# Half 0's four plain up-projection tiles become Strassen steps, with a new order of steps, sums and transfers around them

## The chip, the cores and the metric

The kernel runs on one core of one Trainium2 chip. The metric is the device time of one execution in microseconds, the median of several runs. "The profile" is one profiled execution, read as a page and through views of its trace; times within it count from the start of its span.

## The reference, cut to what matters

One layer of a hybrid encoder on 512 positions of 1024 features. The change touches the last block alone, and there the first product:

```python
x = x + mix @ w_out[l]
h = rms_norm(x, mlp_norm_g[l])                                  # 512 x 1024
x = x + jnp.square(jax.nn.relu(h @ w_up[l])) @ w_down[l]        # 1024 -> 4096 -> 1024
return rms_norm(x, final_norm_g)
```

## The kernel before

Every product is made in three passes, to reach float32 accuracy from fp32r matmuls: each operand is split into a rounded high part and the low part that is left, and `mm3` (L311) adds hi·hi, hi·lo and lo·hi into PSUM. The split of a weight chunk of 128x1024 is two instructions: ScalarE copies the high part (`conv_hi`, L240, instruction at L247), VectorE subtracts it to get the low part (`conv_lo`, L261, at L269). The order on TensorE, ScalarE, VectorE and GpSimd is the written order; SyncE's queue is put in order by a planner, except inside the attention loop.

The up projection runs in two halves of 16 output tiles (`for half in range(2)`, L1513), each followed by its part of the down projection. There are two kinds of tile work:

- A plain tile (`up_tile` L1558, and three tiles together at the start of half 0): 8 k-blocks of three matmuls with 512 columns, then two ReLUs from PSUM on ScalarE and, for every second tile, squares on VectorE (`up_evac`, L1312).
- A group of four tiles done as a 2x2 block product with Strassen's seven products. Each product is a step (`up_step`, L1574) of 8 x 3 matmuls with 256 columns. Steps are named `f0:kind`: 11 and 21 use unsummed weights and unsummed activations; t1, t2, t3 and t4 use sums of weight blocks, and t1, t2, t3 and 22 sums of activation blocks. A group has up to three PSUM banks: a (11, t2, t3, t4), b (21) and c (t1, 22). `quad_evac` (L1372) follows each step: ScalarE copies 11, t1 and t2 out as `v`, VectorE adds `v` and PSUM for t3, 21 and 22; the ReLU and the square come later, on ScalarE for groups in `ON_ACT`.

In half 0 tiles 0 to 3 are plain (`n0` to `n3` in `STEPS`, L54) and the groups 4, 8 and 12 are Strassen groups: 4 tiles and 21 steps. In half 1 all four groups are Strassen groups: 28 steps.

What surrounds the steps, in half 0:

- Weights. Unsummed chunks arrive in three rotating `wraw` buffers; `emit_dma` (L226) loads the next when one is used up. Summed weights live in four rotating `tw` buffers: `load_t` (L1177) loads block 12 through SyncE and adds further blocks with accumulating DMAs from GpSimd's queue (L1181). t1 becomes t2 in place by another accumulating DMA (L277), t3 gets block 22 added by VectorE (L281), and t4 is t2 + 21, added by VectorE (L286). During each step the weights of the third step after it are split (`feed`, L299).
- Activations. `h2_t` (L1207) transposes x1n on TensorE into PSUM, and ScalarE writes the high part h2h and a copy hm; `h2_l` (L1219) subtracts on VectorE. Four of these stand in the output projection (`BES`, L1242 on), four after the first k-block of the plain tiles. `h_sums` (L1330) then makes the four sums on VectorE, 16 instructions in all, and stores them in DRAM for half 1; `h_hi` and `h_lo` (L1356, L1360) split them.
- `x1_sq` (L1266) squares x1n for the norm, eight times in half 0; `scale_neg` (L1546) makes the negated factors. `load_s1` (L1498) brings and adds the first weights of the down projection into `ts`.
- `late` ties such work to a step and a k-block; `op_next` and `next_a` fill in sums and splits of the finished activations for the down projection.

## Time and profile before

| | us |
|---|---|
| Median of 3 runs | 525.5 (525.3 to 525.65) |
| The profiled execution's own time | 525.27 |
| Its span | 523.5 |
| Its mean granted TensorE clock | 0.997 of full speed |
| TensorE, VectorE, ScalarE busy | 516.8, 430.2, 352.3 |

In rows of the trace the columns are start, duration, engine, line, operation, the tiles written and read, and how often. A row that groups instructions has the summed busy time, the mean of one in ns, and the idle time of the engine before them with what ended it. Matmuls overlap in their pipeline: two rows' start times tell more than the durations. L312, L313 and L314 are the three passes of `mm3`. `pu` is PSUM of the up projection, `pd` that of the down projection, `pxt` that of the transposes. The time outside the span is 525.27 - 523.5 = 1.77.

### The profile page before, as it was taken

How to read it: one execution, taken by the hardware profiler on the slowest of the kernel's cores; microseconds unless marked ns; L12 is line 12 of the kernel's file. 1: busy time of each engine (PE TensorE's matmuls, PEld its weight loads, DVE VectorE, ACT ScalarE, POOL GpSimd, SP SyncE). 2: the span in 40 equal slices, each digit the busy share in tenths (PEclk: the TensorE clock that was granted, in tenths of full speed). 3: DMA queues.
4: the chain of work that ended last, by engine and by line, in shares of the span. 5: the costliest groups of instructions: out<-in, count | busy, mean ns of one | idle time of the engine just before them, and what ended most of it. 6: DMA issues, size and time to landing. Idle time of an engine off the chain costs nothing.

```text
span 523.5 us, 8213 instructions
## 1 busy us (share of the span) xinstructions
PE 516.8 (99%) x3021; PEld 443.4 (85%) x3021; DVE 430.2 (82%) x668; ACT 352.3 (67%) x568; POOL 65.8 (13%) x90
## 2 busy tenths in 40 slices
PE   9999999999999999999999999999999999999995
PEld 8857888787787788899999888889999999888884
DVE  6998995888887898898789987789766978986985
ACT  7579946668865847586578656565667577655664
POOL 0182000000000421001300311001100300140000
PEclk9999999999999999999999999999999999999998
DMA  7736545357696499947695899977987497799804
GB/s 288 234 87 196 161 145 180 106 168 216 187 289 208 104 191 268 332 133 192 140 222 149 217 273 275 308 265 162 294 260 172 115 229 208 156 283 257 202 1 162
DMA packets 40329, 105.15 MB, mean 201 GB/s; under 512 B 5056, under 2 KB 13376, under 8 KB 40288
## 3 DMA queue, kind: packets, MB, share of 16 engines
q1 hardware_dynamic: 32448, 78.10, 44.6%
q0 software_dynamic: 7696, 26.32, 27.2%
q8 instruction: 24, 0.39, 0.3%
q10 hardware_dynamic: 144, 0.20, 0.1%
q14 instruction: 17, 0.14, 0.1%
HBM read 95.59 MB, written 4.29 MB: 191 GB/s over the span
## 4 chain that ended last, share of the span: by engine, by line
PE 99%; DVE 0%; issue 0%; DVEq 0%; ACT 0%; ACTq 0%
PE pu L313 10%; PE pu L314 10%; PE pu L312 10%; PE pd L313 10%; PE pd L312 10%; PE pd L314 10%; PE pqk L312 3%; PE pwo L312 3%; PE pqk L314 3%; PE pqk L313 3%; PE pwo L314 3%; PE pwo L313 3%; PE pav L942 2%; PE pt L842 2%; PE ps L806 2%; PE pp L312 1%
## 5 line engine op out<-in xcount | busy, mean ns | idle before, releaser
L269 DVE TENSOR_TENSOR wlo<-wraw,whi 128x1024 fp32r<-128x1024 f32 x71 | 86.5, 1219 | 24.2 <-ACT whi L247 24.0
L247 ACT ACTIVATE whi<-wraw 128x1024 fp32r<-128x1024 f32 x67 | 70.7, 1057 | 37.3 <-PE pd L314 18.2
L313 PE MATMUL pd<-wlo,ah 128*128 128x512 f32 (+1 forms) x195 | 75.2, 386 | 0.0
L312 PE MATMUL pd<-whi,ah 128*128 128x512 f32 (+1 forms) x195 | 75.2, 386 | 0.0
L314 PE MATMUL pd<-whi,al 128*128 128x512 f32 (+1 forms) x195 | 75.2, 386 | 0.0
L314 PE MATMUL pu<-hh,wlo 128*128 128x256 f32 x224 | 63.4, 283 | 0.0
L313 PE MATMUL pu<-hl,whi 128*128 128x256 f32 x224 | 63.4, 283 | 0.0
L312 PE MATMUL pu<-hh,whi 128*128 128x256 f32 x224 | 63.4, 283 | 0.0
L312 PE MATMUL pu<-h2h,whi 128*128 128x256 f32 (+1 forms) x200 | 60.1, 300 | 0.0
L313 PE MATMUL pu<-h2l,whi 128*128 128x256 f32 (+1 forms) x200 | 60.0, 300 | 0.0
L314 PE MATMUL pu<-h2h,wlo 128*128 128x256 f32 (+1 forms) x200 | 60.0, 300 | 0.0
L269 DVE TENSOR_TENSOR wlo<-tw,whi 128x1024 fp32r<-128x1024 f32 x37 | 45.1, 1220 | 17.2 <-ACT whi L247 17.2
L247 ACT ACTIVATE whi<-tw 128x1024 fp32r<-128x1024 f32 x38 | 40.1, 1059 | 25.1 <-PE pd L314 6.3
L247 ACT ACTIVATE whi<-ts 128x1024 fp32r<-128x1024 f32 x24 | 25.5, 1061 | 26.5 <-PE pd L314 18.5
L312 PEld LDWEIGHTS pu<-hh,whi 128*128 128x128 f32 x224 | 43.0, 192 | 0.0
L313 PEld LDWEIGHTS pu<-hl,whi 128*128 128x128 f32 x224 | 43.0, 192 | 0.0
L314 PEld LDWEIGHTS pu<-hh,wlo 128*128 128x128 f32 x224 | 43.0, 192 | 0.0
L312 PEld LDWEIGHTS pd<-whi,ah 128*128 128x128 f32 x195 | 36.6, 188 | 7.4
L314 PEld LDWEIGHTS pd<-whi,al 128*128 128x128 f32 x195 | 36.6, 188 | 7.4
L313 PEld LDWEIGHTS pd<-wlo,ah 128*128 128x128 f32 x195 | 36.6, 188 | 7.3
L312 PEld LDWEIGHTS pu<-h2h,whi 128*128 128x128 f32 x200 | 38.3, 191 | 1.3
L313 PEld LDWEIGHTS pu<-h2l,whi 128*128 128x128 f32 x200 | 38.3, 191 | 1.3
(277 smaller groups left out, 1218.0 us busy)
## 6 DMA issues: line engine op xcount, KB each, us to landing
wraw<-in_w_up_dram SPq DMA_DIRECT2D x25, 512.0 KB, 4.8
ts<-in_w_dn_dram POOLq DMA_DIRECT2D x24, 512.0 KB, 13.1
wraw<-in_w_dn_dram SPq DMA_DIRECT2D x24, 512.0 KB, 8.9
tw<-in_w_up_dram SPq DMA_DIRECT2D x15, 512.0 KB, 6.6
tw<-in_w_up_dram POOLq DMA_DIRECT2D x15, 512.0 KB, 7.9
wraw<-in_w_in_dram SPq DMA_DIRECT2D x13, 512.0 KB, 3.9
ts<-in_w_dn_dram SPq DMA_DIRECT2D x8, 512.0 KB, 7.5
tw<-in_w_dn_dram SPq DMA_DIRECT2D x8, 512.0 KB, 7.5
```

Source lines behind the costliest of these rows:

```text
L247: act(hi, raws[i], AF.Copy)
L269: nc.vector.tensor_tensor(lo, r, f(splits[i][0]), op=OP.subtract)
L312: nc.tensor.matmul(o, lhsT=a[0], rhs=b[0], start=bool(first), stop=False, skip_group_check=on)
L313: nc.tensor.matmul(o, lhsT=a[0], rhs=b[1], start=False, stop=False, skip_group_check=on)
L314: nc.tensor.matmul(o, lhsT=a[1], rhs=b[0], start=False, stop=bool(last), skip_group_check=on)
L806: nc.tensor.matmul(psq[p, u][e][:, :NK], lhsT=qs_[p, a][r, P * qt:P * qt + P], rhs=kks[p][r, b, w:w + NK], start=i == 0, stop=i == 2)
L842: nc.tensor.transpose(pt[:, i * P:(i + 1) * P], en[h][qt][:, k:k + P], ident)
L942: nc.tensor.matmul(pav[p][a, co], lhsT=vs[:, jt, h * DH:(h + 1) * DH], rhs=et[h, jt][:, ci], start=jt == 0 and i == 0, stop=jt == 3 and i ...
```

## The change

- `STEPS[0]` has group 0 in place of the four plain tiles, so half 0 has 28 steps too. Its first six are 11 and 21 of the groups 0, 8 and 4, which need no sums. `up_tile`, `up_evac` and the three tiles at the start go.
- The first step takes its matmuls in another order: for each half of the output hi·hi and lo·hi of all four k-blocks, then the four that read the low activations.
- `h_sums` becomes `h_sum`, tied to steps one by one: the t1 and t2 sums on VectorE, the t3 and 22 sums on GpSimd (12 instructions). The later four transposes stand in the first and second step, in two lots.
- In half 0 all t4 weight sums are accumulating DMAs (`RAW`); group 0's t2 is loaded for itself and its t3 gets block 22 by DMA (`ADDED`); group 12's t3 gets it by VectorE one step later (`more`). `load_t` can leave its adds to `add_t`, at a later step.
- The evacuation of three 21 steps is put off (`later`, `put`); every group's squares are on ScalarE; group 4's bank a moves to other PSUM buffers (`AJ`).
- Four of the eight `x1_sq` and the negated factors move into the down projection. The adds of the first down weights (`add_s1`) stand apart from their loads, in the last steps.
- From the ninth step of half 0 to its last, SyncE's order is the written one.
- The second half of the final gain is loaded in three pieces in place of four (`FGP`).

```diff
 STEPS = (
-    "n0 n1 n2 4:11 4:t1 n3 4:t2 4:21 4:22 4:t3 8:11 8:t1 4:t4 8:21 8:t2 8:22 8:t3 12:11 12:t1 8:t4 12:t2 12:22 12:t3 12:21 12:t4",
+    "0:11 8:11 4:11 0:21 8:21 4:21 0:t1 8:t1 0:t2 0:22 0:t3 8:t2 4:t1 8:22 0:t4 8:t3 4:t2 8:t4 4:22 12:11 4:t3 12:t1 4:t4 12:t2 12:22 12:t3 12:21 12:t4",
     "0:11 0:t1 0:21 0:t2 0:22 0:t3 8:11 8:t1 0:t4 8:21 8:t2 8:22 8:t3 12:11 12:t1 8:t4 12:21 12:t2 12:22 12:t3 4:11 4:t1 12:t4 4:t2 4:22 4:t3 4:21 4:t4")
-QUADS = ((4, 8, 12), (0, 8, 12, 4))
-ON_ACT = {(h, f, k) for h in range(2) for f in QUADS[h] if (h, f) != (0, 4) for k in ("21", "22", "t3", "t4")}
+QUADS = ((0, 8, 4, 12), (0, 8, 12, 4))
+AJ = {(0, 4), (1, 0)}
+ADDED = {(0, 0), (0, 12)}
+RAW = {(0, 0), (0, 4), (0, 8), (0, 12)}
+ON_ACT = {(h, f, k) for h in range(2) for f in QUADS[h] for k in ("21", "22", "t3", "t4")}
...
     for (h, f0, kind), i in cq.items():
-        if kind == "11" and (h, f0) != (0, 4):
+        if kind == "11" and h:
+            swap[i], swap[i + 1] = i + 1, i
+        if (h, f0, kind) == (0, 12, "t2"):
...
                     raws[cq[h, f0, "t2"]] = r
-                elif kind == "22":
+                elif kind == "22" and (h, f0) not in ADDED:
...
                     nc.vector.tensor_tensor(t, t, r, op=OP.add)
+                elif kind == "22" and f0 == 12:
+                    st["r"] = r
+                elif (h, f0) in RAW and kind == "t2":
+                    nc.gpsimd.dma_start(r, ublock(h, "21", f0), accum_op=OP.add)
+                    raws[cq[h, f0, "t4"]] = r
+                elif (h, f0) in RAW and kind == "21":
+                    emit_dma()
...
-    def load_t(half, n, f0):
+    def load_t(half, n, f0, adds=True):
...
         nc.sync.dma_start(t, ublock(half, "12", f0))
-        for b in {"t1": ("11",), "t2": ("11", "22"), "t3": ()}[n]:
-            nc.gpsimd.dma_start(t, ublock(half, b, f0), accum_op=OP.add)
         raws[cq[half, f0, n]] = t
+        if adds:
+            add_t(half, n, f0)
+    def add_t(half, n, f0):
+        for b in {"t1": ("11",), "t2": ("11", "22"), "t3": ("22",) if (half, f0) in ADDED else ()}[n]:
+            nc.gpsimd.dma_start(raws[cq[half, f0, n]], ublock(half, b, f0), accum_op=OP.add)
...
     BES["21"].update({1: lambda: o_lo("s1", 1), 3: lambda: conv_lo(C_WA + 7)})
-    BES["s1"].update({1: lambda: (o_lo("22", 0), o_lo("22", 1), h2_t(0, "gs")), 2: lambda: h2_t(1, "gs"), 3: lambda: (conv_lo(C_WA + 8), h2_l(0))})
-    BES["22"].update({1: lambda: (h2_t(2, "gs"), h2_l(1)), 2: lambda: (h2_t(3, "gs"), conv_lo(C_WA + 9)), 3: lambda: (h2_l(2), h2_l(3))})
+    BES["s1"].update({1: lambda: (o_lo("22", 0), o_lo("22", 1), h2_t(0, "gs")), 2: lambda: h2_t(1, "gs"), 3: lambda: (h2_t(2, "gs"), h2_l(0))})
+    BES["22"].update({0: lambda: h2_l(1), 1: lambda: (h2_t(3, "gs"), h2_l(2)), 2: lambda: (h2_l(3), conv_hi(C_WA + 9)), 3: lambda: None})
...
                 BES[w][i]()
-        if w in ("s3", "s4", "21"):
-            load_t(0, {"s3": "t1", "s4": "t2", "21": "t3"}[w], 4)
+        if w in ("s3", "s4", "21", "s1"):
+            load_t(0, *{"s3": ("t1", 0), "s4": ("t3", 0, False), "21": ("t2", 0), "s1": ("t1", 8)}[w])
...
-    def h_sums(k):
+    def h_sum(n, k):
...
         if k % 2 == 0:
-            for n in SUMS:
-                hsum[n, m] = g_("hsum")
-        a, b = hm.pop(k), hm.pop(k + 4)
-        e, s2, s3, s4 = [hsum[n, m][:, c] for n in SUMS]
-        nc.vector.tensor_tensor(e, b[:, right], a[:, right], op=OP.subtract)
-        stt(s2, a[:, left], -1.0, e, op0=OP.mult, op1=OP.subtract)
-        nc.vector.tensor_tensor(s3, a[:, left], a[:, right], op=OP.subtract)
-        stt(s4, b[:, left], -1.0, s2, op0=OP.mult, op1=OP.subtract)
+            hsum[n, m] = hsr[n, m] = g_("hsum")
+        a, b, o = hm[k], hm.get(k + 4), hsr[n, m][:, c]
+        if n == "t1":
+            nc.vector.tensor_tensor(o, b[:, right], a[:, right], op=OP.subtract)
+        elif n == "t2":
+            stt(o, a[:, left], -1.0, hsr["t1", m][:, c], op0=OP.mult, op1=OP.subtract)
+        elif n == "t3":
+            nc.gpsimd.tensor_tensor(o, a[:, left], a[:, right], op=OP.subtract)
+        else:
+            nc.gpsimd.tensor_tensor(o, a[:, left], b[:, left], op=OP.subtract)
+            nc.gpsimd.tensor_tensor(o, o, hsr["t1", m][:, c], op=OP.add)
         if k % 2:
-            for i, n in enumerate(SUMS):
-                nc.sync.dma_start(hsd[i][:, m * S:(m + 1) * S], hsum[n, m])
+            nc.sync.dma_start(hsd[SUMS.index(n)][:, m * S:(m + 1) * S], hsr[n, m])
+    hsr = {}
...
     HJ = 20
-    FGP = ((0, 32, 64, 128), (0, 32, 64, 96, 128))
+    FGP = ((0, 32, 64, 128), (0, 32, 64, 128))
...
-    def load_s1(half, ts, qs=range(NQ)):
-        for q in qs:
-            t = ts[:, q, :]
-            nc.sync.dma_start(t, wblock(half, "11", q))
-            nc.gpsimd.dma_start(t, wblock(half, "12", q), accum_op=OP.add)
-            raws[cd_[half] + 2 * q + 1] = t
+    def load_s1(half, ts, q):
+        nc.sync.dma_start(ts[:, q, :], wblock(half, "11", q))
+    def add_s1(half, ts, q):
+        t = raws[cd_[half] + 2 * q + 1] = ts[:, q, :]
+        nc.gpsimd.dma_start(t, wblock(half, "12", q), accum_op=OP.add)
...
     for half in range(2):
-        c0, cd = cu.get((half, 0)), cd_[half]
+        cd = cd_[half]
...
         todo = deque((w, q) for _, w, q in seq)
...
-        def scale_neg():
+        def room():
...
             ts = big.tile([P, NQ, 1024], FT, name="ts", tag="bigA")
-            for tt in range(4):
-                nr2[tt] = consts.tile([P, 1], FT, name="nr2_%d" % tt)
-                nc.vector.tensor_scalar(nr2[tt], r2[tt], -1.0, None, op0=OP.mult)
...
             bank, keep = banks.setdefault(f0, {}), keeps.setdefault(f0, {})
-            x = {"t1": "c", "22": "c", "21": "b"}.get(kind, "a")
-            if x not in bank:
-                bank[x] = ps_("pu", {"a": "pj" if (half, f0) == (1, 0) else "gs", "b": "pj", "c": "et"}[x])
+            b = {"t1": "c", "22": "c", "21": "b"}.get(kind, "a")
+            if (half, kind, f0) == (0, "11", 4):
+                banks[0]["b"] = ps_("pu", "pj")
+            if b not in bank:
+                bank[b] = ps_("pu", {"a": "pj" if (half, f0) in AJ else "gs", "b": "pj", "c": "et"}[b])
...
             hi, lo = splits[c]
+            head = half == 0 and (kind, f0) == ("11", 0)
...
                 sl = slice(n * P, (n + 1) * P)
-                mm3(bank[x][:, e * TH:(e + 1) * TH], (hi[:, sl], lo[:, sl]), h_part(kind, k),
-                    n == 0 and kind in ("11", "t1", "21"), n == 7, True)
+                o, w, x, first = bank[b][:, e * TH:(e + 1) * TH], (hi[:, sl], lo[:, sl]), h_part(kind, k), n == 0 and kind in ("11", "t1", "21")
+                if head:
+                    nc.tensor.matmul(o, lhsT=w[0], rhs=x[0], start=first, stop=False, skip_group_check=True)
+                    nc.tensor.matmul(o, lhsT=w[1], rhs=x[0], start=False, stop=False, skip_group_check=True)
+                    for k in range(4) if n % 4 == 3 else ():
+                        sl = slice((4 * e + k) * P, (4 * e + k + 1) * P)
+                        nc.tensor.matmul(o, lhsT=hi[:, sl], rhs=h_part(kind, k)[1], start=False, stop=n == 7 and k == 3, skip_group_check=True)
+                else:
+                    mm3(o, w, x, first, n == 7, True)
...
                     op_next()
-                if n == 6:
+                if n == 6 and (half, kind, f0) != (0, "t2", 12):
                     next_a()
-            quad_evac(kind, f0, bank, keep, (half, f0, kind) in ON_ACT)
+            if half == 0 and kind == "21" and f0 < 12:
+                later.append(lambda: quad_evac("21", f0, bank, keep, True))
+            else:
+                quad_evac(kind, f0, bank, keep, (half, f0, kind) in ON_ACT)
+        later = deque()
+        def put():
+            later.popleft()()
...
                     ts = big.tile([P, NQ, 1024], FT, name="ts", tag="bigA")
-                load_s1(half, ts, (q,))
+                load_s1(half, ts, q)
+                if half:
+                    add_s1(half, ts, q)
...
         qs = QUADS[half]
-        for f0, f1 in zip(qs, qs[1:]):
+        for f0, f1 in zip(qs, qs[1:]) if half else ():
...
         if half == 0:
-            late.update({(4, "11", 0): split_h("t2", 0), (4, "11", 5): split_h("t2", 1), (4, "t1", 1): split_h("22", 0), (4, "t1", 6): split_h("22", 1),
-                         (3, 1): split_h("t3", 0), (3, 6): split_h("t3", 1),
-                         (4, "t1", 4): xt(0, 1), (3, 3): xt(1, 0), (4, "21", 4): xt(1, 1), (4, "t2", 4): xt(2, 0), (4, "22", 4): xt(2, 1),
-                         (4, "t3", 4): xt(3, 0), (8, "11", 5): xt(3, 1), (8, "21", 5): scale_neg})
+            def more():
+                t, r = raws[cq[0, 12, "t3"]], st.pop("r")
+                nc.vector.tensor_tensor(t, t, r, op=OP.add)
+            def sums(*a):
+                return lambda: [h_sum(n, k) for n, k in a]
+            def turn(js):
+                def run():
+                    for j in js:
+                        h2_t(j, "et" if j < 6 else "pj")
+                        h2_l(j)
+                return run
+            late.update({(0, "11", 0): lambda: conv_lo(C_WA + 8), (0, "11", 3): lambda: conv_lo(C_WA + 9), (0, "11", 6): turn((4, 5)), (8, "11", 1): turn((6, 7)),
+                         (0, "11", 1): sums(*[("t3", k) for k in range(4)]), (8, "11", 0): sums(("t1", 0), ("t1", 1)), (8, "11", 5): split_h("t1", 0),
+                         (4, "11", 0): sums(("t1", 2), ("t1", 3), ("22", 0), ("22", 1), ("22", 2), ("22", 3)),
+                         (4, "11", 1): split_h("t1", 1), (0, "21", 0): sums(("t2", 0), ("t2", 1)),
+                         (0, "21", 5): split_h("t2", 0), (8, "21", 0): sums(("t2", 2), ("t2", 3)), (8, "21", 5): split_h("t2", 1),
+                         (4, "21", 5): split_h("22", 0), (0, "t1", 5): split_h("22", 1),
+                         (0, "t3", 3): put, (8, "t2", 3): put, (8, "t1", 1): split_h("t3", 0), (0, "t2", 1): split_h("t3", 1),
+                         (8, "21", 2): lambda: load_t(0, "t1", 4, False), (4, "21", 2): lambda: add_t(0, "t1", 4), (8, "11", 7): lambda: add_t(0, "t3", 0),
+                         (8, "t1", 5): lambda: load_t(0, "t3", 8),
+                         (8, "t2", 6): lambda: load_t(0, "t3", 4), (0, "t4", 3): put, (8, "t3", 0): lambda: load_t(0, "t1", 12, False), (4, "t2", 2): lambda: add_t(0, "t1", 12),
+                         (4, "t3", 0): lambda: load_t(0, "t3", 12, False), (12, "t1", 7): more,
+                         (0, "22", 7): xt(0, 0), (8, "t2", 7): xt(0, 1), (8, "22", 7): xt(1, 0), (4, "t2", 5): xt(1, 1), (4, "22", 5): room,
+                         (12, "t1", 5): lambda: add_s1(half, ts, 0), (12, "t2", 5): lambda: add_s1(half, ts, 1), (12, "22", 5): lambda: add_s1(half, ts, 2), (12, "t3", 5): lambda: add_s1(half, ts, 3)})
...
         if half == 0:
-            late[8, "t3", 4], late[12, "11", 4], late[12, "t2", 1], late[12, "t2", 7] = [load_1(q) for q in range(4)]
+            late[4, "t3", 4], late[12, "11", 4], late[12, "t2", 1], late[12, "t2", 7] = [load_1(q) for q in range(4)]
...
             late[12, "t3", 4], late[4, "11", 4], late[4, "t2", 1], late[4, "t2", 7] = [load_1(q) for q in range(4)]
-        for kind, f0 in up_steps(half)[start:]:
+        for n, (kind, f0) in enumerate(up_steps(half)):
+            if half == 0 and n == 8:
+                sp = tc.manual_schedule(engines={nc.sync.engine})
+                sp.__enter__()
...
             st["step"] = st.get("step", 0) + 1
-            if kind == "n":
-                up_tile(f0, late)
-            else:
-                up_step(kind, f0, late)
+            up_step(kind, f0, late)
+        if half == 0:
+            sp.__exit__(None, None, None)
...
                 load_s3(half, q)
+            if half == 0 and j < 4:
+                x1_sq(2 + j // 2, j % 2)
+                nr2[j] = consts.tile([P, 1], FT, name="nr2_%d" % j)
+            if half == 0 and j == 4:
+                for tt in range(4):
+                    nc.vector.tensor_scalar(nr2[tt], r2[tt], -1.0, None, op0=OP.mult)
...
```

## The prediction

> **What bounds the kernel now.** I read the page first, for the share of each engine and the chain that ended last, then the busy time of the two up-projection stages, then TensorE's order of time at their edges.

> ```profile
> span 523.5 us, 8213 instructions
> PE 516.8 (99%) x3021; PEld 443.4 (85%) x3021; DVE 430.2 (82%) x668; ACT 352.3 (67%) x568; POOL 65.8 (13%) x90
> PE 99%; DVE 0%; issue 0%; DVEq 0%; ACT 0%; ACTq 0%
> ...
> 200.30:284.20 83.90, 83.90 (x616) 79.98 (x615) 71.31 (x107) 56.41 (x92) 6.94 (x8) 1.00 0.73 205
> 360.20:441.60 81.40, 81.40 (x677) 81.28 (x676) 62.20 (x68) 53.89 (x74) 8.64 (x10) 1.00 0.79 208
> ```

> The reader sees one chain, TensorE from end to end. The two last rows are the up-projection of half 0 and of half 1: span, busy time of PE, PEld, DVE, ACT and POOL, granted clock (1.00), DMA share. TensorE never idles there, so only fewer or shorter matmuls gain anything, and every other engine has room: VectorE 85% and 76%, ScalarE 67% and 66%.

> The start times of matmuls, not their modelled durations, give the price of a step.

> ```profile
> 200.30 0.40 PE L312 MATMUL pu<-h2h,whi 128*128 128x512 f32 x1
> ...
> 202.35 1.95 PE L1214 MATMUL pxt<-ident,x1n 128*128 128x128 f32 x16
> 204.06 0.48 PE L312 MATMUL pu<-h2h,whi 128*128 128x512 f32 x1
> 204.37 0.40 PE L313 MATMUL pu<-h2l,whi 128*128 128x512 f32 x1
> ...
> 284.37 0.40 PE L312 MATMUL pd<-whi,ah 128*128 128x512 f32 x1
> ...
> 360.55 0.28 PE L312 MATMUL pu<-h2h,whi 128*128 128x256 f32 x1
> ...
> 441.19 0.40 PE L312 MATMUL pd<-whi,ah 128*128 128x512 f32 x1
> ```

> Half 1 is already 28 Strassen steps: 441.19 - 360.55 = 80.64, or 2.88 a step, 24 matmuls of 256 columns at 0.120. Half 0 runs from 200.30 to 284.37 = 84.07: four plain tiles, 21 steps and 16 transposes. The steps are 60.48; the transposes take 204.06 - 202.35 = 1.71 and their next matmul 0.31 in place of 0.23; what is left for four plain tiles is 21.8, or 5.45 each (0.227 a matmul).

> **The change part by part.** *Matmuls.* Four plain tiles (21.8) become seven steps (20.16): -1.61 by the same difference taken without rounding, 84.07 - 80.64 - 1.82 for the transposes. This is on the path and is all that can be gained. The transposes are split into two lots of eight: one more restart, +0.08.

> *The first steps.* 0:11 now starts where n0 did and needs the fourth low part h2l. TensorE's first eight matmuls use only high parts, so the low parts are asked for at 200.30 + 8 x 0.12 = 201.26, the fourth at 201.6.

> ```profile
> 200.39 0.70 ACT L1217 ACTIVATE hm<-pxt,vt 128x512 f32<-128x512 f32 x1
> ...
> 201.64 0.75 DVE L1204 SCALAR_TENSOR_TENSOR x1n<-pwo,nrc,x 128x512 f32<-128x512 f32 x1
> ...
> L269 DVE TENSOR_TENSOR wlo<-wraw,whi 128x1024 fp32r<-128x1024 f32 x13 | 15.9, 1220 | 4.6 <-ACT whi L247 4.5
> L1387 DVE TENSOR_TENSOR a<-v,pu 128x512 f32<-128x512 f32 x9 | 6.1, 680 | 0.8 <-PE pu L314 0.7
> L1361 DVE TENSOR_TENSOR hl<-hsum,hh 128x512 fp32r<-128x512 f32 x8 | 5.2, 683 | 0.0
> L1220 DVE TENSOR_TENSOR h2l<-hm,h2h 128x512 fp32r<-128x512 f32 x7 | 4.7, 688 | 2.1 <-ACT hm L1217 2.1
> L286 DVE TENSOR_TENSOR tw<-tw,wraw 128x1024 f32<-128x1024 f32 x3 | 3.7, 1219 | 0.0
> L1320 DVE TENSOR_TENSOR a<-a 128x512 f32<-128x512 f32 x4 | 2.6, 684 | 0.0
> L1398 DVE SCALAR_TENSOR_TENSOR a<-a 128x512 f32<-128x512 f32 x3 | 2.1, 693 | 0.1
> L1337 DVE TENSOR_TENSOR hsum<-hm 128x256 f32<-128x256 f32 x4 | 1.7, 418 | 0.0
> ```

> Its source hm is there at 200.39 + 0.70 = 201.1, its subtraction takes 0.69: 201.8, so about +0.15. Behind it on VectorE stands the last x1n, which the moved transposes need at the seventh eighth of 0:11 (about 202.7): 201.8 + 0.75 = 202.5, in time.

> The two weight splits that stood in the output projection (1.22 each, VectorE) are moved into 0:11, behind that x1n. The tightest point is then 4:21, the sixth step. It starts at 200.30 + 0.15 + 5 x 2.88 + 2 x 0.86 of transposes = 216.6. Up to its low weights VectorE must do, from 201.1: five h2l (3.4), one x1n (0.75), five wlo (6.1), four sums for t1 (1.7), two hl (1.4), together 13.4, ready about 214.5, 215.1 with the waits for ScalarE. Slack 1.5. The steps before it have 0.8 (8:11) to 3 (8:21). So the new head hides, if nothing is added to VectorE; I put +0.2 for small misses.

> *Sums of activations by GpSimd.* Four sums for t3 and eight instructions for "22" leave VectorE (8 x 0.42 = 3.4 off it) and become twelve 128x256 tensor_tensors on GpSimd. No row has one of that size. The tiny ones show what matters:

> ```profile
> 29.51 0.20 POOL L163 TENSOR_TENSOR pl<-pl,z 128x8 f32<-128x8 f32 x1
> 30.12 0.53 POOL L163 TENSOR_TENSOR pl<-pl,z 128x8 f32<-128x8 f32 x1
> 30.74 0.73 POOL L164 TENSOR_SCALAR pl<-pl 128x8 f32<-128x8 f32 x1
> ...
> 30.63 0.75 DVE L504 SCALAR_TENSOR_TENSOR xc<-xr,vt,xc 128x511 f32<-128x511 f32 x1
> 31.42 0.75 DVE L505 SCALAR_TENSOR_TENSOR xc<-xr,vt,xc 128x511 f32<-128x511 f32 x1
> 32.09 0.74 DVE L503 SCALAR_TENSOR_TENSOR xc<-xr,vt,xc 128x510 f32<-128x510 f32 x1
> 32.87 0.75 DVE L504 SCALAR_TENSOR_TENSOR xc<-xr,vt,xc 128x511 f32<-128x511 f32 x1
> ```

> Beside VectorE instructions with two operands in SBUF the same GpSimd instruction grows from 0.20 to 0.53 to 0.73: it waits its turn. VectorE starts come 0.67 or 0.78 apart, so a turn costs it about 0.11. Bounds for a 128x256 one: 0.24 (as the tiny ones) to 0.84 (twice VectorE's 0.418); I take 0.6. What VectorE loses lies between nothing (they fall in its waits) and all twelve, 7.2. The likeliest case takes nothing more than the 0.2 above, since the first four read only hm of the first transposes and may run before the low weights are asked for, and the t2 and 22 parts are used only from the ninth step.

> [...]

> *The rest of half 0.* VectorE: +3 weight splits (3.7), +3 evacuations (2.0), less the squares of plain tiles (2.6), the squares now on ScalarE (2.8), the sums (3.4) and three t4 sums that become DMAs (3.7), less about 1 of moved scalars: 71.3 - 7.8 = 63.5 of 82.5, 77%. ScalarE: three weight copies, three v, six relu-and-square pairs more, less eight relus and four squares of x1n moved into the down projection:

> ```profile
> L247 ACT ACTIVATE whi<-wraw 128x1024 fp32r<-128x1024 f32 x12 | 12.8, 1070 | 2.3 <-PE pu L313 1.6 <-ACT scr L1269 0.7
> L1377 ACT ACTIVATE v<-pu 128x512 f32<-128x512 f32 x9 | 5.5, 606 | 6.3 <-PE pu L314 6.3
> L1396 ACT ACTIVATE a<-a 128x512 f32<-128x512 f32 x5 | 3.2, 632 | 0.2
> L1269 ACT ACTIVATE scr<-x1n 128x512 f32<-128x512 f32 x8 | 5.0, 629 | 0.0
> L1317 ACT ACTIVATE a<-pu 128x256 f32<-128x256 f32 x8 | 2.5, 389 | 1.0 <-PE pu L314 1.0
> ```

> about 56.4 + 8 = 64 of 82.5, 78%. Half 1 hides the same steps at 76% and 66%, so on the average nothing shows: 0. The price without that cover is the 1.1 to 1.2 of one split for each step that is late.

> *Transfers and queues.* Each group's t4 sum, and t2 and t3 of group 0, become accumulating DMAs on POOL: eight more of 512 KB. POOL issues in order, so an add that waits for its load holds those behind it; SP in written order does the same.

> ```profile
> DMA to landing us min/median/max: 4.6/6.6/9.8
> ...
> DMA to landing us min/median/max: 5.3/8.8/13.3
> ...
> DMA to landing us min/median/max: 5.4/5.4/7.9
> ...
> tw<-in_w_up_dram POOLq DMA_DIRECT2D x2, 512.0 KB, 6.5
> ```

> These are the loads of line 1179, the adds of 1181, those of 277, and the adds between 230 and 240. The late one is group 12. With step s starting at 202.2 + 2.88 s, its t1 buffer is free when 8:t4 is split, at 202.2 + 14 x 2.88 + 0.7 + 2.3 = 245.5; load 5.0, add 6.5, two conversions 2.3, add 5.4, conversions 2.3 end at 267.0; 12:t2 starts at 268.4. Slack 1.4 by those; by the medians of 6.6 and 8.8 it is 2.5 late; by the minima 3 early. I take 0, the middle of the two ends. While a transfer is late ScalarE waits, and evacuations and copies behind it.

> Moved squares and scale factors go to the first four turns of the down projection, where ScalarE is under two thirds busy; the four w_down adds go to the last steps, and one final-gain load is dropped: 0.

> Sum: -1.61 + 0.08 + 0.15 + 0.2 = -1.2. Against the profiled execution's 525.27 that is 524.1; the median shown is 0.23 higher, so 524.3.

> **The rivals.** *VectorE and GpSimd take turns in the head.* Four t3 sums and four of the 22 sums fall before the low weights of 4:21: 8 x 0.6 = 4.8, less the slack of 1.5 and 0.7 spent in VectorE's own waits: 2.6 late at 4:21, 526.9, slower. It decides from the point where more than 1.5 is lost before 4:21. For it: the rows at 30 us, and a full VectorE there; against it: sums that may run early.

> *The add of group 12 is late.* Half of the 2.5 by medians, 1.3: 525.6, no change. For it: the medians; against it: half 1 has the same pairs and its longest wait for such a transfer is short and hidden:

> ```profile
> ACT whi L247 <- DMA tw<-in_w_up_dram: 4.8, 2, 2.6
> ```

> *SyncE's written order or the POOL queue holds a load back,* so that the saving is not reached and several steps wait: both stalls together and one more, 3.7, 528.0. Against it: buffers of raw weights are still asked for three chunks ahead.

> **How the numbers follow.** What this kernel's measurement can tell from no change is about 0.2%, 1.05. Chances: forecast 0.48 (524.3), first rival 0.25 (526.9), second 0.17 (525.6), third 0.10 (528.0). Faster by over 0.2% is below 524.45: 0.43 of the first case and 0.02 of the second rival where the add comes early, 0.45. Slower, above 526.55: 0.20 + 0.03 + 0.10 = 0.33. The rest, 0.22, lies between. The full saving with no miss is 523.9, so the range starts at 523.8; it ends at 527.6, which leaves out most of the last case. The forecast's own range is 523.8 to 525.0.

> **What would show it.** TensorE from the first to the last up matmul of half 0 should be 82.5 to 82.9 in place of 84.07. If the first rival holds, GpSimd's sums read 0.6 or more, VectorE's starts spread beside them, and TensorE waits at 4:21 for wlo. If the second holds, TensorE waits at 12:t1 or 12:t2, and ScalarE's whi waits for a tw transfer over 4. A stall-free half 0 with a time above 525 would make the prediction wrong elsewhere: in the down projection, where I priced everything at nothing.

## The result, and the profile after

The changed kernel takes **535.07 us** (median of 5 runs, 532.46 to 535.23) against 525.6 (525.3 to 526.15) for the kernel before on the same chip: 1.0168 times, 95% interval 1.0154 to 1.0182. It is slower by 9.5 us, and the forecast of 524.3 and its range were wrong. The profiled execution took 534.54, its span is 532.5.

In the changed kernel the three passes of `mm3` are L320 to L322, the first step's matmuls L1545 to L1549, a weight's high and low part L248 and L270. First the page: span, busy time of the engines, and the chain that ended last.

```profile
span 532.5 us, 8398 instructions
...
PE 519.0 (97%) x3093; PEld 447.6 (84%) x3093; DVE 429.5 (81%) x655; ACT 361.4 (68%) x581; POOL 82.6 (16%) x109
...
PE 82%; DMA 6%; DVE 5%; issue 3%; ACT 2%; POOL 0%; DVEq 0%; ACTq 0%; POOLq 0%; SPq 0%
```

The chain was TensorE from end to end; now 6% of it is a transfer, 5% VectorE, 2% ScalarE. The new kernel's busy time does not tell where; what TensorE waited for between 200 and 297 does (engine, tile and line, what it waited for; us in total, times, the longest):

```profile
PE pd L320 <- ACT a L1383: 3.6, 1, 3.6
PE pu L320 <- DVE a L1386: 1.3, 2, 1.1
PE pu L1549 <- DVE h2l L1232: 1.3, 2, 1.1
PE pu L322 <- DVE wlo L270: 0.7, 1, 0.7
```

The kernel before had none of these four. The up projection's first matmul starts at 201.00 and the first of the down projection at 287.84, 86.84 where 82.5 was forecast, so 4.3 of stalls, not quite half of the loss (between starts a stall costs somewhat more than the wait shown: 4.2 for the four that follow, against 3.3 above). They are, in order: 1.8 in the first step for the low activations h2l, 0.8 at 4:21 for its low weights, 0.4 and 1.2 for two evacuations (the moving of a result out of PSUM) at 240 and 256. The largest stands behind them, in the second turn of the down projection:

```profile
289.00 0.39 PE L322 MATMUL pd<-whi,al 128*128 128x512 f32 x1
292.95 0.79 PE L320 MATMUL pd<-whi,ah 128*128 128x512 f32 x1 [3.56 <-ACT a L1383]
```

And it costs twice. Rows by stretch are: span, busy time of PE, PEld, DVE, ACT, POOL, the granted clock, the DMA share, GB/s.

```profile
288.90:292.90 4.00, 0.49 (x3) 0.06 (x1) 3.52 (x5) 3.94 (x8) 0.85 (x1) 1.00 1.06 236
293.00:295.00 2.00, 2.00 (x5) 1.62 (x6) 1.97 (x4) 1.97 (x4) 0.00 (x0) 0.50 1.06 213
295.00:297.00 2.00, 2.00 (x8) 1.57 (x7) 1.97 (x4) 2.00 (x5) 0.00 (x0) 0.65 1.05 231
297.00:299.00 2.00, 2.00 (x10) 1.64 (x9) 2.00 (x4) 1.78 (x5) 0.00 (x0) 1.00 1.02 307
```

After the wait the granted clock is 0.50: the next eight matmuls start 0.43 apart in place of 0.23, which takes another 1.7. The sum over the kernel: matmuls 82.5 - 84.07 = -1.6, stalls in the up projection +4.3, the wait at its end +3.7, slow clock +1.7, and +0.7 that is already there at the first up matmul (201.00 against 200.30). It is there from the kernel's first loads on, in code that the change leaves alone: the first matmul into the tile `pcs` starts at 21.09 against 20.37. That is +8.8 of 532.5 - 523.5 = 9.0. After 300 the two run alike.

**Why ScalarE's ReLU was 3.6 late.** ScalarE works in the written order. The copy ahead of that ReLU for which it waited, and the ReLU (six instructions between them are left out); then SyncE's issues before them; then SyncE's longest wait; then GpSimd's issue of the additions:

```profile
287.52 1.06 ACT L248 ACTIVATE whi<-ts 128x1024 fp32r<-128x1024 f32 x1 [6.66 <-DMA ts<-in_w_dn_dram]
292.32 0.58 ACT L1383 ACTIVATE a<-pu 128x512 f32<-128x512 f32 x1
```
```profile
257.49 0.43 SPq L1498 DMA_DIRECT2D ts<-in_w_dn_dram  x1
257.97 1.20 SPq L1187 DMA_DIRECT2D tw<-in_w_up_dram  x1
272.67 0.33 SPq L229 DMA_DIRECT2D wraw<-in_w_dn_dram  x1
273.04 1.27 SPq L1498 DMA_DIRECT2D ts<-in_w_dn_dram  x2
```
```profile
SPq L229 <- DVE tw L1598: 13.4, 1, 13.4
```
```profile
279.90 2.62 POOL L1502 DMA_DIRECT2D ts<-in_w_dn_dram  x3 [7.89 <-DMA ts<-in_w_dn_dram]
```

From 259 to 272.67 SyncE stands 13.4 at a `wraw` load whose buffer comes free only when VectorE has done `more`, the t3 sum of group 12. Two loads of `ts` stand behind it in the written order although their own place is free. They leave at 273.04. One of them is the first of the four: in the new order its place, 4:t3, stands one step behind that of the second, 12:11, which left at 257.49. GpSimd adds in the order of use, so the addition of the second, long loaded, waits behind the first too, and three go out together at 279.90. ScalarE waits 6.66 for the first sum, and the ReLU that frees the PSUM bank stands behind that copy in its order. The planner of the kernel before had issued all four at 202.41.

**Why the first step and 4:21 stalled.** The groups of VectorE and of GpSimd beside it, from 200.6 to 219 (count, busy, mean ns of one, idle before it), and from 199 to 219:

```profile
L1232 DVE TENSOR_TENSOR h2l<-hm,h2h 128x512 fp32r<-128x512 f32 x6 | 8.1, 1382 | 0.0
L270 DVE TENSOR_TENSOR wlo<-wraw,whi 128x1024 fp32r<-128x1024 f32 x5 | 6.8, 1392 | 0.8 <-ACT whi L248 0.8
L1360 DVE TENSOR_TENSOR hl<-hsum,hh 128x512 fp32r<-128x512 f32 x2 | 1.8, 911 | 0.7 <-ACT hh L1357 0.7
```
```profile
L1338 POOL TENSOR_TENSOR hsum<-hm 128x256 f32<-128x256 f32 x4 | 4.3, 1081 | 3.3 <-ACT hm L1229 3.3
L1339 POOL TENSOR_TENSOR hsum<-hsum 128x256 f32<-128x256 f32 x4 | 3.7, 932 | 4.0 <-DVE hsum L1332 3.8
L1336 POOL TENSOR_TENSOR hsum<-hm 128x256 f32<-128x256 f32 x4 | 3.1, 1059 | 0.0
```

An h2l subtraction takes 1382 ns where it took 688, a weight split 1392 where it took 1220, a split of sums 911 where it took 683: VectorE is held up while GpSimd's sums run, and a sum on GpSimd takes 0.93 to 1.08 (means).

**Why two evacuations stalled.** ScalarE's longest wait for summed weights in half 0:

```profile
237.33 1.06 ACT L248 ACTIVATE whi<-tw 128x1024 fp32r<-128x1024 f32 x1 [3.54 <-DMA tw<-in_w_up_dram]
```

With two more such waits, at 232.25 (2.47) and 240.54 (0.58), ScalarE has 6.6 less and works from there to 257 without a break, so its copies come late. At 253 VectorE waits 1.39 for one of them, adds a t3 sum (1.22) and only then makes the `a` that frees the bank at 256. The transfers are full meanwhile (share 1.06 from 232 to 240).

### The profile page after: what moved, and what is told of

Its sections match the earlier page's. It is cut to its first block, busy times and chain, and to the rows that moved or that the text cites. A ratio compares the mean times of both kernels' runs of the same rounds, so it can differ in the third digit from the quotient of the medians.

```text
span 532.5 us, 8398 instructions
## 1 busy us (share of the span) xinstructions
PE 519.0 (97%) x3093; PEld 447.6 (84%) x3093; DVE 429.5 (81%) x655; ACT 361.4 (68%) x581; POOL 82.6 (16%) x109
## 4 chain that ended last, share of the span: by engine, by line
PE 82%; DMA 6%; DVE 5%; issue 3%; ACT 2%; POOL 0%; DVEq 0%; ACTq 0%; POOLq 0%; SPq 0%
PE pd L320 10%; PE pd L322 9%; PE pd L321 9%; PE pu L320 6%; PE pu L322 6%; PE pu L321 6%; DMA tw<-in_w_up_dram 4%; PE pqk L320 3%; PE pqk L322 3%; PE pqk L321 3%; PE pwo L320 3%; PE pwo L322 2%; PE pwo L321 2%; PE pav L950 2%; PE pt L850 2%
## 5 line engine op out<-in xcount | busy, mean ns | idle before, releaser
L270 DVE TENSOR_TENSOR wlo<-wraw,whi 128x1024 fp32r<-128x1024 f32 x70 | 86.1, 1233 | 23.9 <-ACT whi L248 23.7
L248 ACT ACTIVATE whi<-wraw 128x1024 fp32r<-128x1024 f32 x66 | 69.3, 1054 | 35.2 <-PE pd L322 17.6
L320 PE MATMUL pd<-whi,ah 128*128 128x512 f32 (+1 forms) x195 | 75.9, 389 | 3.6 <-ACT a L1383 3.6
L322 PE MATMUL pd<-whi,al 128*128 128x512 f32 (+1 forms) x195 | 75.7, 388 | 0.0
L320 PE MATMUL pu<-hh,whi 128*128 128x256 f32 x256 | 72.5, 283 | 0.3 <-DVE a L1386 0.3
L321 PE MATMUL pu<-hl,whi 128*128 128x256 f32 x256 | 72.4, 283 | 0.0
L322 PE MATMUL pu<-hh,wlo 128*128 128x256 f32 x256 | 72.4, 283 | 0.0
L270 DVE TENSOR_TENSOR wlo<-tw,whi 128x1024 fp32r<-128x1024 f32 x41 | 50.1, 1221 | 23.3 <-ACT whi L248 23.3
L248 ACT ACTIVATE whi<-tw 128x1024 fp32r<-128x1024 f32 x42 | 44.3, 1056 | 24.7 <-DMA tw<-in_w_up_dram 10.9
L320 PE MATMUL pu<-h2h,whi 128*128 128x256 f32 x184 | 52.2, 284 | 1.1 <-DVE a L1386 1.1
L322 PE MATMUL pu<-h2h,wlo 128*128 128x256 f32 x184 | 52.2, 284 | 0.7 <-DVE wlo L270 0.7
L321 PE MATMUL pu<-h2l,whi 128*128 128x256 f32 x184 | 52.1, 283 | 0.0
L320 PEld LDWEIGHTS pu<-hh,whi 128*128 128x128 f32 x256 | 49.1, 192 | 0.4 <-ACT whi L248 0.4
L321 PEld LDWEIGHTS pu<-hl,whi 128*128 128x128 f32 x256 | 49.1, 192 | 0.0
L322 PEld LDWEIGHTS pu<-hh,wlo 128*128 128x128 f32 x256 | 49.1, 192 | 0.0
L320 PEld LDWEIGHTS pd<-whi,ah 128*128 128x128 f32 x195 | 36.9, 189 | 11.2 <-ACT a L1383 4.0
L248 ACT ACTIVATE whi<-ts 128x1024 fp32r<-128x1024 f32 x24 | 25.4, 1059 | 30.1 <-PE pd L322 15.8
L322 PEld LDWEIGHTS pd<-whi,al 128*128 128x128 f32 x195 | 36.9, 189 | 7.6
L270 DVE TENSOR_TENSOR wlo<-ts,whi 128x1024 fp32r<-128x1024 f32 x24 | 29.3, 1223 | 16.2 <-ACT whi L248 16.1
L320 PEld LDWEIGHTS pu<-h2h,whi 128*128 128x128 f32 x184 | 35.3, 192 | 1.3 <-ACT a L1394 1.3
## 6 DMA issues: line engine op xcount, KB each, us to landing
wraw<-in_w_up_dram SPq DMA_DIRECT2D x24, 512.0 KB, 4.9
wraw<-in_w_dn_dram SPq DMA_DIRECT2D x24, 512.0 KB, 9.6
ts<-in_w_dn_dram POOLq DMA_DIRECT2D x24, 512.0 KB, 11.8
tw<-in_w_up_dram POOLq DMA_DIRECT2D x22, 512.0 KB, 7.7
tw<-in_w_up_dram SPq DMA_DIRECT2D x17, 512.0 KB, 6.6
wraw<-in_w_in_dram SPq DMA_DIRECT2D x13, 512.0 KB, 4.2
ts<-in_w_dn_dram SPq DMA_DIRECT2D x8, 512.0 KB, 6.3
tw<-in_w_dn_dram SPq DMA_DIRECT2D x8, 512.0 KB, 7.3
```

Of the source, the lines that this page charges most:

```text
L248: act(hi, raws[i], AF.Copy)
L270: nc.vector.tensor_tensor(lo, r, f(splits[i][0]), op=OP.subtract)
L320: nc.tensor.matmul(o, lhsT=a[0], rhs=b[0], start=bool(first), stop=False, skip_group_check=on)
L321: nc.tensor.matmul(o, lhsT=a[0], rhs=b[1], start=False, stop=False, skip_group_check=on)
L322: nc.tensor.matmul(o, lhsT=a[1], rhs=b[0], start=False, stop=bool(last), skip_group_check=on)
```

## The experiments

Each is the changed kernel with the edit shown (lines are cut to what changes), and computes the whole reference. Times are medians; the kernel before lay at 526.11, 525.48, 525.61 and 525.77 in the four lots (e1 to e4, e5 to e7, e8 to e10, e11 and e12).

| kernel | us | against before, 95% |
|---|---|---|
| e1 first ts load earlier | 528.28 | 1.0044 (1.0028 to 1.0059) |
| e2 sums on VectorE | 533.5 | 1.0150 (1.0121 to 1.0179) |
| e3 planner's order | 530.9 | 1.0098 (1.0060 to 1.0136) |
| e4 = e1 + e2 | 528.41 | 1.0046 (1.0032 to 1.0059) |
| e5 e4, sums later | 525.77 | 0.9999 (0.9988 to 1.0011) |
| e6 e5 with GpSimd's sums | 527.9 | 1.0044 (1.0031 to 1.0057) |
| e7 e5 with the planner's order | 529.16 | 1.0071 (1.0057 to 1.0084) |
| e8 e5, two squares later | 524.93 | 0.9988 (0.9975 to 1.0002) |
| e9 e5, stores later | 531.11 | 1.0101 (1.0071 to 1.0130) |
| e10 = e8 + e9 | 530.83 | 1.0092 (1.0070 to 1.0113) |
| e11 e8, stores in two lots | 527.74 | 1.0035 (1.0022 to 1.0048) |
| e12 e8, four stores later | **524.31** | **0.9970 (0.9958 to 0.9982)** |

**e1: one load earlier in SyncE's order.** The first `ts` load moves from 4:t3 (step 20) to 12:11 (step 19), one step and not the two that the expectation says.

```diff
-            late[4, "t3", 4], late[12, "11", 4], late[12, "t2", 1], late[12, "t2", 7] = [load_1(q) for q in range(4)]
+            late[12, "11", 3], late[12, "11", 4], late[12, "t2", 1], late[12, "t2", 7] = [load_1(q) for q in range(4)]
```

> The load of the first w_down sum is put two steps earlier in SyncE's written order, ahead of the wraw load that waits for group 12's t3 sum. Theory, order of the SyncE queue: the 6.7 us that ScalarE waited for ts and the 3.6 us TensorE stood at the second pd accumulation go, and with them the half clock after it, about 1.8: 535.07 - 5.5 = 529.6. Rival, transfers are too slow altogether: the wait only moves to another transfer, 533 or more.

The first two `ts` loads now leave together, ahead of the blocked one:

```profile
257.18 0.90 SPq L1498 DMA_DIRECT2D ts<-in_w_dn_dram  x2
```

The wait at the down projection is gone, and with it the slow clock there (the down projection's first 24 matmuls start 0.22 to 0.24 apart). The time falls by 6.8 us (6.5 by the ratios, 5.9 between the two profiled executions). This is the larger part of the loss, from one line of the order.

**e2: the twelve sums on VectorE, at the same places.**

```diff
-            nc.gpsimd.tensor_tensor(o, a[:, left], a[:, right], op=OP.subtract)
+            nc.vector.tensor_tensor(o, a[:, left], a[:, right], op=OP.subtract)
...
-            nc.gpsimd.tensor_tensor(o, a[:, left], b[:, left], op=OP.subtract)
-            nc.gpsimd.tensor_tensor(o, o, hsr["t1", m][:, c], op=OP.add)
+            nc.vector.tensor_tensor(o, a[:, left], b[:, left], op=OP.subtract)
+            nc.vector.tensor_tensor(o, o, hsr["t1", m][:, c], op=OP.add)
```

> The twelve sums for t3 and 22 run on VectorE at the same places, the same twelve instructions. Theory, GpSimd and VectorE take turns: h2l and wlo go back to 0.69 and 1.22 each, the first step's stall falls from 1.8 to about 0.2, about 533; VectorE gains only about 1 us by it, since the sums themselves take it 4.3. Rival, VectorE is simply full in the head: 4:21 comes later still, 535 or more.

VectorE's h2l subtractions from 200 to 226:

```profile
L1232 DVE TENSOR_TENSOR h2l<-hm,h2h 128x512 fp32r<-128x512 f32 x6 | 3.9, 685 | 0.4 <-ACT hm L1229 0.4
```

They are back at 685 from 1382, and the first step no longer waits for h2l, so GpSimd's sums were what stalled it. But 4:21 now waits 2.6 for its weights: the work did not go, it moved. The end stays nearly as it was (3.0).

**e3: SyncE left to the planner** (the two lines that enter and leave the written order are taken out).

> SyncE is not put in order by hand in half 0; all else as changed. Theory, queue order: the ts loads are issued before group 12's t3 sum again and the stall at the down projection goes, 529 to 530. Rival: the planner's order delays weight loads in the up projection, and the sum is no better than 533.

The wait at the down projection goes here too, so it was the written order. But ScalarE waits 8.6 in all for `tw` transfers in half 0, and the up projection takes 88.8. So written order is worth something: only one of its lines was wrong.

**e4: e1 and e2 together.**

> Both edits of the first two runs. Theory, two causes apart from each other: the gains add, 527 to 528. Rival, one cause behind both: no better than the better one of the two.

Nothing gained on e1 (the intervals overlap), though only one wait is left, 2.4 at 4:21. Two views tell why. VectorE's rows ahead of that split, and the stretches around the wait:

```profile
214.76 0.42 DVE L1338 TENSOR_TENSOR hsum<-hm 128x256 f32<-128x256 f32 x1
...
217.60 0.42 DVE L1339 TENSOR_TENSOR hsum<-hsum 128x256 f32<-128x256 f32 x1
217.94 0.68 DVE L1360 TENSOR_TENSOR hl<-hsum,hh 128x512 fp32r<-128x512 f32 x1
218.54 1.22 DVE L270 TENSOR_TENSOR wlo<-wraw,whi 128x1024 fp32r<-128x1024 f32 x1
```
```profile
217.00:220.00 3.00, 0.57 (x5) 0.36 (x4) 2.97 (x6) 0.89 (x1) 0.00 (x0) 1.00 0.52 195
220.00:222.00 2.00, 2.00 (x14) 2.00 (x14) 2.00 (x4) 1.54 (x2) 0.00 (x0) 0.76 0.61 143
222.00:225.00 3.00, 3.00 (x17) 3.00 (x17) 3.00 (x6) 2.17 (x5) 0.73 (x1) 0.59 0.90 309
```

Eight instructions for the 22 sums, needed four steps later, and a split for t1 stand ahead of the split that TensorE waits for: 3.8 from 214.76 to 218.54. And a wait of 2.4 is followed by 3.4 us at half clock, about 1.5 more. Together that is nearly the whole excess, 86.5 against 82.5.

**e5: the sums ordered by when they are needed.** On e4: the 22 sum is one instruction as before the change (this line of `h_sum` is not shown); t1 sums in one lot, their splits behind the weights of 4:21, 22 and t3 sums two and five steps later.

```diff
-(0, "11", 1): sums(*[("t3", k) for k in range(4)]), (8, "11", 0): sums(("t1", 0), ("t1", 1)), (8, "11", 5): split_h("t1", 0),
-(4, "11", 0): sums(("t1", 2), ("t1", 3), ("22", 0), ("22", 1), ("22", 2), ("22", 3)),
-(4, "11", 1): split_h("t1", 1),
+(4, "21", 1): sums(*[("t3", k) for k in range(4)]), (8, "11", 3): sums(*[("t1", k) for k in range(4)]), (4, "11", 5): split_h("t1", 0),
+(8, "21", 3): sums(("22", 0), ("22", 1), ("22", 2), ("22", 3)),
+(4, "11", 6): split_h("t1", 1),
```

> The changed kernel with the load of the first ts moved behind 12:11 as in e1, all sums of activations on VectorE, t3 and 22 as one instruction each, and placed later: t1 sums in one lot in 8:11, its splits behind the weights of 4:21, 22 sums at 8:21, t3 sums at 4:21. My theory (VectorE's written order puts work with a late deadline ahead of the low weights of 4:21): no stall of more than 0.3 in half 0, TensorE's up phase 82.6 to 83.5, time 524.2 to 525.2. Rival (the raw weights of the first steps arrive too late, since the transfers are full there): VectorE is idle behind ScalarE and the wraw load, TensorE still waits 1 to 2.5 at 4:21, with a stretch of half clock behind it; 526 to 528.

The head has no stall left. In the profiled execution (524.31) one wait of 0.5 remains, for an evacuation at 251. But the runs spread from 523.98 to 527.49 and their median is above what was expected: not faster than before.

**e6: the same places, t3 and 22 sums on GpSimd.**

> The same places as e5, with the t3 and 22 sums (twelve instructions) left on GpSimd. My theory of turns: GpSimd's instruction takes about 1.06 where VectorE is busy and costs VectorE about 0.46 each, so VectorE loses 5.5 in the steps 4 to 7 where e5 spends 3.4 on the same sums; it has slack there, so half 0 is 82.6 to 84.5 and the time 524.5 to 526.5, not below e5 by more than 0.3. Rival (only the place in the order mattered, GpSimd's sums are free): mean of VectorE's hl and wlo stays 0.68 and 1.22 beside them, and e6 is 0.3 to 1 below e5 or the same with VectorE 3 us less busy.

2.1 us slower than e5, and above the range expected. VectorE from 200 to 226, then its slowest split and GpSimd's rows beside it:

```profile
L270 DVE TENSOR_TENSOR wlo<-tw,whi 128x1024 fp32r<-128x1024 f32 x3 | 7.0, 2340 | 0.0
L270 DVE TENSOR_TENSOR wlo<-wraw,whi 128x1024 fp32r<-128x1024 f32 x5 | 6.9, 1436 | 0.0
L1232 DVE TENSOR_TENSOR h2l<-hm,h2h 128x512 fp32r<-128x512 f32 x6 | 4.6, 777 | 1.1 <-ACT hm L1229 1.1
L1360 DVE TENSOR_TENSOR hl<-hsum,hh 128x512 fp32r<-128x512 f32 x4 | 3.7, 953 | 0.0
L1332 DVE TENSOR_TENSOR hsum<-hm 128x256 f32<-128x256 f32 x4 | 2.5, 692 | 0.0
L1334 DVE SCALAR_TENSOR_TENSOR hsum<-hm,hsum 128x256 f32<-128x256 f32 x4 | 2.0, 550 | 0.0
```
```profile
223.00 4.59 DVE L270 TENSOR_TENSOR wlo<-tw,whi 128x1024 fp32r<-128x1024 f32 x1
...
223.37 3.12 POOL L1336 TENSOR_TENSOR hsum<-hm 128x256 f32<-128x256 f32 x4
```

The mean of 2340 hides two splits at 1.21 and 1.22 and one at 4.59: that one stood until four sums of GpSimd in a row were done (226.49) and ended 1.10 later. Against 1220, 688, 683 and 418 for the same shapes undisturbed the six groups lose 3.4 + 1.1 + 0.5 + 1.1 + 1.1 + 0.5 = 7.7; e5 does the same sums on VectorE in eight instructions of 0.42, 3.4. Giving them to GpSimd takes from VectorE more than it saves. The expected 5.5 was too low.

**e7: e5 with SyncE left to the planner.**

> e5 with SyncE's order left to the planner in place of the written one (and the ts load where the change has it). If the written order is worth something by itself (as e3 against e1 suggests, 2.6): ScalarE waits for tw transfers, TensorE 1 to 2 in half 0, time 1 to 3 above e5. If e3's stalls came from the head alone: within 0.5 of e5.

3.4 us above e5, with waits of 5.3 in all in half 0: the written order is worth that much, once its one fault is mended.

**e8 to e10: why e5 spreads.** In e5's profile ScalarE waits four times, 4.6 in all, for `tw` transfers between 226 and 240, then works without a break until 254, and a PSUM bank comes free too late. Either the backlog is shortened (two squares of 0.8 go to steps 20 and 22, e8), or the transfers are relieved (the eight stores of sums, 2 MB, wait until after the load of group 12's t3, e9), or both (e10).

```diff
-(8, "22", 7): xt(1, 0), (4, "t2", 5): xt(1, 1),
+(4, "t3", 2): xt(1, 0), (4, "t4", 2): xt(1, 1),
```
```diff
-            nc.sync.dma_start(hsd[SUMS.index(n)][:, m * S:(m + 1) * S], hsr[n, m])
+            stored.append(lambda d=hsd[SUMS.index(n)][:, m * S:(m + 1) * S], t=hsr[n, m]: nc.sync.dma_start(d, t))
...
+(4, "t3", 1): lambda: [f() for f in stored],
```

> e5 with two of the four x1_sq left in half 0 (0.8 of ScalarE each) moved from steps 13 and 16 to steps 20 and 22, where ScalarE waits for TensorE 1.4 and 1.5. My theory of e5's rest: ScalarE waits 4.6 in all for tw transfers between 226 and 240, then works without a break from 239 to 254 and writes group 12's first bank free 0.5 late, more in runs with later transfers. Then the backlog is 1.6 shorter, the stall at 251 goes and the median falls by 0.5 to 1, to 524.6 to 525.2. Rival (the late transfer itself, not the backlog): the same as e5 within 0.4.

> e5 with the eight 256 KB stores of the sums (2 MB, read again only in the second half of the down projection) put off from 209 to 224 to after the load of group 12's t3 at 254. Theory: the transfers are full from 200 to 240 (share 0.82 to 1.06), and 2 MB less there brings the tw weights earlier: ScalarE's waits for tw fall from 4.6 to under 2.5, the median by 0.5 to 1, to 524.6 to 525.2. Rival (the latency of an accumulating transfer, not the load of the engines): waits for tw stay over 4 and the time within 0.4 of e5; or the stores now stand before the ts adds and the pd start stalls again by 0.5 or more.

> Both edits. If both theories hold: no stall over 0.3, up phase 82.5 to 82.8, 524.0 to 524.8 and a spread below 1; if only one does, as that one.

e8 alone: 524.93, still from 523.7 to 527.71, so the backlog is only part of it. The stores are the instructive miss. ScalarE's waits from 200 to 265 and the stretch from 210 to 220, in e8:

```profile
ACT whi L248 <- DMA tw<-in_w_up_dram: 5.5, 3, 2.6
```
```profile
210.00:220.00 10.00, 10.00 (x86) 10.00 (x85) 8.36 (x16) 7.00 (x10) 0.00 (x0) 1.00 0.82 284
```

The same views of e10:

```profile
ACT v L1375 <- DMA hsd<-hsum: 4.7, 1, 4.7
...
ACT whi L248 <- DMA tw<-in_w_up_dram: 0.8, 3, 0.4
```
```profile
210.00:220.00 10.00, 10.00 (x86) 10.00 (x85) 8.94 (x18) 7.78 (x11) 0.00 (x0) 1.00 0.58 196
```

Without the stores the transfers are at 0.58 in place of 0.82, ScalarE's waits for them fall from 5.5 to 0.8, and no stall is left before 265. So what the weights waited for was, in the main, the other traffic. e9 shows it less clearly: its profile has 3.6 of such waits where e5's has 4.6 and under 2.5 was expected; with the stores moved otherwise they are 1.7 (e11) and 1.8 (e12) before 265. But the stores hold their buffers: at 259 the next evacuation needs one and waits 4.7 for a store (9.0 in e9, whose TensorE then waits 6.8). The relief was right and the place wrong.

**e11 and e12: the stores at a better place.** e11 puts four to step 15 and four to step 19; e12 leaves those of t1 and t2 where they were and puts only those of 22 and t3 to step 15. e12's edit against e10:

```diff
+            if n in ("t1", "t2"):
+                stored.popleft()()
...
-(4, "t3", 1): lambda: [f() for f in stored],
+(8, "t3", 1): store(4),
```

> e8 with the stores in two lots: the four of t1 and t2 at step 15 (about 244), the four of 22 and t3 at step 19 (about 254). Theory from e10 (with the stores gone, the waits for tw fell from 5.5 to 0.8 and no stall was left before 265; what stalled there was an evacuation waiting 4.7 for its buffer, still held by a store): with the first lot ten us earlier the buffers come free in time, no stall over 0.3 in half 0, up phase 82.5 to 82.9, 523.8 to 524.6, spread below 1.5. Rival: the second lot is still too late, or the first delays the load and add for 12:t1: a stall of 0.5 to 2 after 255, 525 to 526.5.

> e8 with the four stores of t1 and t2 where e8 has them and those of 22 and t3 at step 15 (about 244). The transfers between 217 and 226 carry 1 MB less, half of e10's relief: waits for tw between 0.8 and 5.5, 523.9 to 525; no wait for a buffer held by a store. If the whole 2 MB have to go for the relief: within 0.4 of e8 (524.9).

In e11 the second four went to SyncE ahead of the load of group 12's t3 (its issue row moves from 252.57 in e12 to 257.52); ScalarE waited 3.4 not for that load but for the addition that makes group 12's t2 (L278), which left at 258.78 and took 8.6 to land, against 257.23 and 6.9 in e12; whether the stores made it so slow is not shown. TensorE then waited 1.8 for ScalarE, and half clock followed: the rival's stall, and a time above its 525 to 526.5. In e12 TensorE waits for nothing between 200 and 297:

```profile
span 522.1 us, 8382 instructions
...
PE 515.4 (99%) x3093; PEld 446.0 (85%) x3093; DVE 426.6 (82%) x663; ACT 361.7 (69%) x581; POOL 71.8 (14%) x97
```
```profile
200.38 0.28 PE L1546 MATMUL pu<-h2h,whi 128*128 128x256 f32 x1
...
282.93 0.40 PE L320 MATMUL pd<-whi,ah 128*128 128x512 f32 x1
```

82.55 from first to last, and five runs from 523.84 to 524.42: as expected (523.9 to 525), and faster than both kernels, 0.9970 of before (0.9958 to 0.9982).

## Why the prediction was wrong, step by step

- **Matmuls, -1.61 and +0.08: right.** e12's 82.55 is the forecast's 82.5. The saving was there; the change as written lost 10.4 elsewhere.
- **"Transfers and queues … I take 0" and "the four w_down adds go to the last steps … 0": this step failed most**, 5.4 of the 9. I followed group 12's weights through SyncE and GpSimd, but not what stands behind them: the `ts` loads queue after a `wraw` load that waits for `more`. The diff shows it; no row of the trace of before could, since there the loads leave at 202.41. The third rival names the mechanism, "SyncE's written order … holds a load back", at 0.10 and 3.7. Its place was the end of the half, not the steps. The argument against it, raw buffers asked for three chunks ahead, was the cause: the load ahead is the one that blocks. e1 shows it. Its 3.7 was no sum of its own parts either: 2.6 and 1.3 are more already.
- **"The likeliest case takes nothing more" for GpSimd's sums: failed.** 0.6 a sum was 0.93 to 1.08, above the upper bound of 0.84, and VectorE did not lose nothing but about 5.5 from 200.6 to 219. The first rival had this as a loss at 4:21 of 2.6; it came as 1.8 in the first step and 0.8 at 4:21; that the sum is the same is chance, since its terms hold nothing of the first step. What I had wrong was the order: the t3 sums may run early, but "early" was beside the h2l subtractions on which the first step hangs, 0.15 in my sum and 1.8 measured. Beside GpSimd's sums an h2l subtraction took 1382 ns against 688, and in e6 a split 4.59 us against 1.22. The bounds from the tiny GpSimd rows did not hold; and of these rows 0.20 and 0.53 are one instruction, while 0.73 is another (L164, which takes 0.24 at 29.80).
- **"Half 1 hides the same steps … 0" for the rest of half 0: failed by 1.7.** An average of 77% and 78% does not show a wait for one transfer (measured: VectorE 67.2 of 86.8, 77%, with the 5.5 lost to GpSimd in it; ScalarE 59.9, 69%). The second rival expected the late transfer at group 12; it came at 232 to 240, long before, and what stalled TensorE was not the weights but the evacuations behind them. e10 and e12 show that the traffic, in the main, made them late.
- **The clock: left out.** The wait's price was taken as its length. Here 1.7 came on top, and in e4 about 1.5.
- The 0.7 at the start is not explained. The profiles of the twelve kernels, with the same code there, have their first up matmul between 200.25 and 201.19, so it is probably no effect of the change; it was not tried.

## What to carry to other kernels

When an order is written by hand, follow each queue past the change: for every instruction that can wait, list what stands behind it and when that is due, to the end of the stage and into the next. Sort the work of an engine that follows the written order by when its result is needed, not by when its input is there (e5 has no wait at 4:21, e4 one of 2.4); and moving the sums from a full VectorE to GpSimd was no relief here (e6: VectorE's instructions beside them lost 7.7 for 3.4 saved). A load that comes late may be late because of other traffic (e8 and e10: without the stores the share of the transfers fell from 0.82 to 0.58 and the waits for them from 5.5 to 0.8), and a store that is put off keeps its buffer (4.7 of waiting for one, e10): both ends have to be looked up before it moves.

## What the runs showed of the hardware that was not expected

After TensorE waited 3.56 (the changed kernel), 2.61 and 3.04 (e2), 2.43 (e4), 2.46 (e10) and 1.81 (e11), the granted clock was 0.50 for 3.41 us, and after 6.80 (e9) for twice that; 1.5 to 1.7 was lost on top of the wait. In e11 the 17 matmuls from 277.43 to 281.06 start 0.21 apart in place of 0.12, which is 1.6 on top of 1.81: that wait cost nearly twice its length.

```profile
274.23:277.64 3.41, 1.60 (x13) 1.40 (x12) 2.63 (x3) 3.41 (x7) 0.00 (x0) 1.00 1.04 199
277.64:281.06 3.42, 3.42 (x18) 3.42 (x18) 2.71 (x4) 2.66 (x4) 0.00 (x0) 0.50 1.03 270
```
```profile
242.77:246.18 3.41, 1.80 (x16) 1.63 (x15) 2.00 (x3) 0.74 (x1) 0.00 (x0) 1.00 0.33 66
246.18:249.59 3.41, 2.24 (x17) 2.04 (x18) 3.34 (x7) 3.38 (x6) 0.00 (x0) 1.00 0.70 214
249.59:253.01 3.42, 3.42 (x31) 3.42 (x30) 3.19 (x4) 3.36 (x8) 0.85 (x1) 1.00 0.80 248
```

e11's wait lies in one stretch, 1.81 idle of 3.41, and the next is at half clock; e7's two waits lie on both sides of a mark, 1.61 and 1.17 idle, and nothing falls. In these runs a stretch with 1.81 idle or more always cost the next one, and 1.61 or less did not, with two exceptions: 1.50 in the head of e1 and 1.39 in that of e3 did. Both of these end in 0.2 to 0.3 of transposes; whether that is the reason is not shown. The changed kernel's head, with 1.27 idle in its stretch, kept the clock. So e7's 2.78 of waits, on the two sides of a mark, cost no slow clock, and e11's 1.81 within one stretch did.
